# FFN up projections of a two-layer trunk: norm and block sums per tile on VectorE, weights by 128 columns two pairs ahead

## The chip, the cores and the metric

One NeuronCore of a Trainium2 chip runs the whole program. The metric is the device time of one execution in microseconds; the kernel before has a median of 2,806.35 us over three runs (2,805.0 to 2,806.55).

## The reference

The input is a residual stream of 1,024 tokens with 1,024 features, all float32. Layer 0 mixes tokens with multi-head latent attention (MLA), layer 1 with a gated MLP over chunks of 128 tokens (gMLP). Each is followed by a squared-ReLU feed-forward network (FFN) and a gated embedding (PLE):

```python
for i in range(DEPTH):                       # DEPTH = 2
    hn = rms_norm(h, norm_mix[i])
    mix = mla_mixer(hn, ...) if i == 0 else gmlp_mixer(hn, ...)
    h = h + mix                              # both end in a product with w_out
    hn = rms_norm(h, norm_ffn[i])
    h = h + jnp.square(jax.nn.relu(hn @ ffn_w_up[i])) @ ffn_w_down[i]
    hn = rms_norm(h, norm_ple[i])
    h = h + jax.nn.sigmoid(hn @ ple_w_gate[i]) * (p[i] @ ple_w_proj[i])
```

`ffn_w_up[i]` is 1,024 x 4,096, `mla_w_out` 1,024 x 1,024, `gmlp_w_out` 2,048 x 1,024. `rms_norm` divides by the root of the mean square over the features and multiplies by a gain.

## The kernel before

The residual stream stands feature-major: `h[k]`, k = 0 to 7, holds features 128k to 128k+127 of all 1,024 tokens (128 x 1024). Every product is made of three: both factors are split into a rounded part (`hi`, a cast on ScalarE, called ACT below) and the rest (`lo`, a subtraction on VectorE, DVE), and TensorE (PE) adds hi x hi, hi x lo and lo x hi. `split` does both halves; its cast is L111, its subtraction L112. The names of an operand end in h and l, those of weights are `wh` and `wl`.

**Output projections.** `down_slice` (L537) goes over four groups q of 256 output columns. `load_block` fetches the weights of a group (512 KB) and splits them, then two tiles f = 0, 1 of 128 columns are computed and added to `h[j]` in PSUM eviction on DVE (L545). Two of these calls feed an FFN: the second half of the MLA projection, `wo1` (results `wo10` to `wo17`), and the last slice of the gMLP projection, `go3` (results `go30` to `go37`). After each second tile `NormX.add_pair` (L275) makes what the up projection needs of it.

**Up projections.** They use a scheme of seven products for a 2 x 2 block product. The blocks of the right side are made from `h[2q]` and `h[2q+1]` times the gain, each cut into two halves of 512 tokens: `B11`, `B21`, `B22` and the combinations `T1` to `T4`, all split into hi and lo. GpSimd (POOL) makes one difference and adds the squares for the norm (L304) into `n_acc`. `rest` splits what of T3 and T4 isn't made early. The weights come as 16 pairs of 128 columns: `wino_weights` (L340) loads a pair as two blocks of 4 k tiles x 256 columns (`wx_r`, 512 KB each, pieces of 1,024 bytes), makes eight sums on POOL of 128x256 (L356, L359, L362, L365), and splits seven operands `wx_A..` and `wx_S..`. `wino_up` runs `pair(n)` for n = 0 to 15, with `run(i)` for product i of seven, each 12 matmuls; the results are called `f0u3g` and `f0u3y` for the first layer's pair 3. The banks are x and z (`g`) and y; a result is copied out of a bank on ACT (`u`, L443) before the next product is added to it. In pair 0 the sums of squares become the norm's factor: `nrm.sums` splits `n_acc` (`n_shl`, L209 and L210), PE adds it up over partitions (`f0u0st`), `nrm.roots` makes `n_rb`. Each finished row of 128 is stored to `apark` in DRAM and read back for the down projection.

**What sets the order.** Each engine has one queue which runs in order. A scheduler writes the queues out ahead of time, by the code's order, dependences, free slots in the pools (`pr` for raw weights, `pw` and `ph` for splits, `pt` for temporaries) and a lead `LEAD`. `up_first` draws the first operands of pair 0's weights while the projection ahead of it still runs (`after(j)`).

Of the kernel before, what the change touches and what calls it, by code (L numbers as in the profile page):

```python
# [40 lines left out]
def trunk(ctx: ExitStack, tc: tile.TileContext, I, out):  # L41
# [218 lines left out]
    class NormX(Norm):  # L260


        def __init__(self, name, gains, place, early):
# [6 lines left out]
        def put(self, c, q, src):  # L270
            hi, lo = self.place(self.name, c, q)
            split(hi, lo, src)
            self.x[c][q] = (hi, lo)

        def add_pair(self, q, h):  # L275
            n = f"{self.name}_{q}"
            u = [tmp(f"{n}u{e}", [P, 2, 512]) for e in range(2)]
            for e in range(2):
                S.activation(u[e].rearrange("p c t -> p (c t)"), h[2 * q + e], AF.Copy, scale=self.g[2 * q + e])
            a = tmp(f"{n}a", [P, 2, 512])  # L280
            b = pw.tile([P, 2, 512], F32, tag="w", name=f"{n}b")
            G.tensor_tensor(a[:, 0], u[0][:, 1], u[0][:, 0], op=ALU.subtract)
            V.tensor_tensor(b[:, 0], u[1][:, 1], u[0][:, 1], op=ALU.subtract)
            self.put("B21", q, u[1][:, 0])
            self.put("B11", q, u[0][:, 0])
            V.tensor_tensor(a[:, 1], u[1][:, 1], a[:, 0], op=ALU.subtract)
            self.put("T1", q, a[:, 0])
            V.tensor_tensor(b[:, 1], u[1][:, 0], a[:, 1], op=ALU.subtract)
            self.put("T2", q, a[:, 1])
            self.put("B22", q, u[1][:, 1])  # L290
            for c, src in (("T3", b[:, 0]), ("T4", b[:, 1])):
                if c in self.early:
                    self.put(c, q, src)
                else:
                    self.kept[c, q] = src
            for e in range(2):
                k = 2 * q + e
                if self.acc is None:
                    self.acc = pb.tile([P, T], F32, tag="acc", name=f"{self.name}_acc")
                    S.activation(self.acc, h[k], AF.Square)  # L300
                else:
                    sq = tmp(f"{n}sq{e}")
                    S.activation(sq, h[k], AF.Square)
                    G.tensor_tensor(self.acc, sq, self.acc, op=ALU.add)  # L304
                nc.sync.dma_start(self.hpark[k], h[k])

        def rest(self):
            for c in ("T3", "T4"):
                for q in range(4):
                    if (c, q) in self.kept:  # L310
                        self.put(c, q, self.kept.pop((c, q)))
# [26 lines left out]
    wslot = [0]  # L338

    def wino_weights(w, f0):  # L340
# [4 lines left out]
        for j in range(2):  # L345
            r = pr.tile([P, 4, 256], F32, tag="raw", name=f"{name}r{j}")
            nc.sync.dma_start(r, w[j * 512:(j + 1) * 512, f0:f0 + 256].rearrange("(k p) f -> p k f", p=P))
            raw.append(r.rearrange("p (q e) (g f) -> p q e g f", e=2, g=2))

        def quad(j, e, g):  # L350
            return raw[j][:, :, e, g, :]

        sa, sb = (ph.tile([P, 2, 4, 128], F32, tag="h", name=f"{name}s{x}") for x in "ab")
        for j in range(2):
            js = slice(2 * j, 2 * j + 2)
            G.tensor_tensor(sa[:, 0, js], quad(j, 0, 1), quad(j, 1, 1), op=ALU.add)  # L356
        for j in range(2):
            js = slice(2 * j, 2 * j + 2)
            G.tensor_tensor(sa[:, 1, js], sa[:, 0, js], quad(j, 0, 0), op=ALU.subtract)  # L359
        for j in range(2):  # L360
            js = slice(2 * j, 2 * j + 2)
            G.tensor_tensor(sb[:, 0, js], quad(j, 1, 0), sa[:, 1, js], op=ALU.subtract)  # L362
        for j in range(2):
            js = slice(2 * j, 2 * j + 2)
            G.tensor_tensor(sb[:, 1, js], quad(j, 0, 0), quad(j, 0, 1), op=ALU.subtract)  # L365
        for what in ("A12", "A11", "S1", "S2", "S4", "S3", "A22"):
            wslot[0] = (wslot[0] + 1) % 12
            pool, tag = (ph, "h") if wslot[0] % 12 < 4 else (pw, "w")
            t = pool.tile([P, 2, 4, 128], F32R, tag=tag, name=f"{name}{what}")
            if what[0] == "A":  # L370
                e, g = int(what[2]) - 1, int(what[1]) - 1
                for j in range(2):
                    js = slice(2 * j, 2 * j + 2)
                    split(t[:, 0, js], t[:, 1, js], quad(j, e, g))
            else:
# [1066 lines left out]
```

## Time and profile before

| | before |
|---|---|
| median of three runs | 2,806.35 us |
| profiled execution: time, span | 2,807.97 us, 2,806.2 us |
| TensorE (PE) matmul, busy | 2,654.2 us, 95% |
| VectorE (DVE) busy | 1,461.8 us, 52% |
| ScalarE (ACT) busy | 1,050.4 us, 37% |
| GpSimd (POOL) busy | 598.4 us, 21%, 738 instructions |
| mean granted TensorE clock | 0.975 |

The profiled execution is one run with the hardware profiler on; its time lies 1.8 us above its span, and it lies 1.6 us above the median of the others. Busy shares are means over the whole span. The strips of the page show each engine in 40 slices of the span, a digit being the busy share in tenths; PEclk is the clock that TensorE was granted, in tenths of full speed.

### The profile page before, as it was taken

What the parts mean: (1) busy time and instruction counts of PE and PEld (TensorE: products, weight loads), DVE (VectorE), ACT (ScalarE), POOL (GpSimd) and SP (SyncE); (2) the same over time, 40 slices, a digit from 0 to 9 for tenths busy, and PEclk for the clock granted to TensorE, in tenths of its full rate; (3) what the DMA queues carried; (4) which work ended last, traced back from release to release, by engine and by line L of the source; (5) the groups of instructions that cost most, each with busy time, mean ns of one, the idle gap of its engine ahead of it and who ended that gap; (6) DMA issues with size and microseconds to landing.
All of it is one profiled execution on the core that took longest, in us unless ns stands there. A gap on an engine that the chain in (4) does not pass through costs nothing. (4 is left out here: it accounts for less than half of the span.)

```text
span 2806.2 us, 34481 instructions
## 1 busy us (share of the span) xinstructions
PE 2654.2 (95%) x13216; PEld 2224.5 (79%) x13216; DVE 1461.8 (52%) x2336; ACT 1050.4 (37%) x2191; POOL 598.4 (21%) x738
## 2 busy tenths in 40 slices
PE   8999998689999999999999999995799999999999
PEld 7898986467777888888888787884577778888899
DVE  6777774565545444375523534435745555444652
ACT  4677762344434122154522221213543443211341
POOL 4544331342330000001211422213433310000000
PEclk9999999789999999999999999997899999999999
DMA  4100011123326333232233311311223254322221
GB/s 161 55 17 31 2 53 60 60 90 105 113 91 230 101 105 113 64 96 74 95 110 104 90 50 58 93 34 68 83 91 119 91 177 168 113 91 69 85 83 35
DMA packets 174262, 247.51 MB, mean 88 GB/s; under 512 B 9057, under 2 KB 135585, under 8 KB 174097
## 3 DMA queue, kind: packets, MB, share of 16 engines
q1 hardware_dynamic: 169280, 230.21, 25.2%
q0 software_dynamic: 4816, 15.10, 1.7%
q8 instruction: 104, 1.70, 0.3%
q14 instruction: 62, 0.50, 0.1%
HBM read 186.55 MB, written 58.72 MB: 87 GB/s over the span
## 5 line engine op out<-in xcount | busy, mean ns | idle before, releaser
L111 ACT CAST wh<-raw 128x1024 fp32r<-128x1024 f32 x96 | 101.0, 1052 | 321.7 <-PE f0d L65 115.9
L112 DVE TENSOR_TENSOR wx_A<-wx_r,wx_A 128x256 fp32r<-128x256 f32 x192 | 99.2, 552 | 116.9 <-ACT wx_A L111 116.2
L356 POOL TENSOR_TENSOR wx_sa<-wx_r 128x256 f32<-128x256 f32 x64 | 53.4, 835 | 454.7 <-DMA wx_r<-in_ffn_w_up_dram 301.0
L112 DVE TENSOR_TENSOR wl<-raw,wh 128x1024 fp32r<-128x1024 f32 x96 | 122.9, 1280 | 48.8 <-ACT wh L111 42.4
L545 DVE TENSOR_TENSOR f0h<-f0d,f0h 128x512 f32<-128x512 f32 (+1 forms) x84 | 70.3, 865 | 145.8 <-PE f0d L65 145.7
L545 DVE TENSOR_TENSOR f1h<-f1d,f1h 128x512 f32<-128x512 f32 (+1 forms) x84 | 70.3, 865 | 139.4 <-PE f1d L65 139.4
L614 POOL TENSOR_TENSOR f0h<-sig,f0h 128x512 f32<-128x512 f32 x16 | 21.9, 1387 | 487.4 <-DVE sig L613 470.2
L65 PE MATMUL go<-yh,wh 128*128 128x512 f32 x256 | 89.6, 418 | 22.6 <-ACT wh L111 22.6
L65 PE MATMUL go<-yh,wl 128*128 128x512 f32 x256 | 87.6, 409 | 9.3 <-DVE wl L112 9.3
L545 DVE TENSOR_TENSOR f0h<-go,f0h 128x512 f32<-128x512 f32 (+1 forms) x52 | 40.6, 810 | 103.4 <-PE go L65 103.4
L111 ACT CAST wx_A<-wx_r 128x256 fp32r<-128x256 f32 x192 | 70.9, 404 | 58.5 <-DMA wx_r<-in_ffn_w_up_dram 37.7
L764 ACT ACTIVATE u<-up,n_r 128x512 f32<-128x512 f32 x32 | 22.0, 688 | 189.1 <-PE up L65 189.1
L65 PE MATMUL go<-yl,wh 128*128 128x512 f32 x256 | 88.5, 413 | 0.0
L755 POOL TENSOR_TENSOR vr<-vr,gb 128x512 f32<-128x512 f32 x32 | 44.0, 1392 | 188.5 <-DVE vr L754 188.5
L694 DVE BATCH_NORM_STATS2 vst<-vg 128x6 f32<-128x512 f32 (+1 forms) x40 | 23.2, 586 | 110.5 <-ACT vg L693 110.5
L65 PEld LDWEIGHTS go<-yh,wh 128*128 128x128 f32 x256 | 51.3, 202 | 34.7 <-ACT wh L111 23.9
L65 PE MATMUL s<-kT,q 128*128 128x512 f32 (+5 forms) x288 | 73.1, 357 | 2.3 <-DVE q L112 1.8
L112 DVE TENSOR_TENSOR wx_S<-wx_sa,wx_S 128x512 fp32r<-128x512 f32 x64 | 56.1, 880 | 35.0 <-ACT wx_S L111 34.0
L693 ACT ACTIVATE vg<-vp,n_r 128x512 f32<-128x512 f32 (+1 forms) x40 | 23.8, 603 | 120.3 <-PE vp L65 118.9
L65 PE MATMUL av<-pt,v 128*128 128x256 f32 (+1 forms) x480 | 64.0, 283 | 5.0 <-DVE sm L1238 2.4
L1239 POOL TENSOR_SCALAR p<-p,sm 128x128 f32<-128x128 f32 (+3 forms) x64 | 49.2, 769 | 88.3 <-DVE sm L1238 58.1
L65 PEld LDWEIGHTS go<-yh,wl 128*128 128x128 f32 x256 | 50.5, 199 | 21.8 <-DVE wl L112 11.5
(5241 smaller groups left out, 8431.1 us busy)
## 6 DMA issues: line engine op xcount, KB each, us to landing
wx_r<-in_ffn_w_up_dram SPq DMA_DIRECT2D x64, 512.0 KB, 4.8
raw<-in_ffn_w_down_dram SPq DMA_DIRECT2D x56, 512.0 KB, 3.5
f0ar<-f_apark SPq DMA_DIRECT2D x32, 512.0 KB, 4.0
f1ar<-f_apark SPq DMA_DIRECT2D x32, 512.0 KB, 4.2
raw<-in_ffn_w_down_dram SPq DMA_DIRECT2D x32, 256.0 KB, 2.9
raw<-in_ple_w_gate_dram SPq DMA_DIRECT2D x16, 512.0 KB, 3.9
vr<-vpark SPq DMA_DIRECT2D x16, 512.0 KB, 4.0
raw<-in_gmlp_w_out_dram SPq DMA_DIRECT2D x16, 512.0 KB, 3.5
```

The source lines that it names most:

```text
L65: PE.matmul(o, l, r, start=start, stop=stop)
L111: S.copy(hi, src)
L112: V.tensor_tensor(lo, src, f32(hi), op=ALU.subtract)
L356: G.tensor_tensor(sa[:, 0, js], quad(j, 0, 1), quad(j, 1, 1), op=ALU.add)
L545: V.tensor_tensor(h[j][:, c], u, h[j][:, c], op=ALU.add)
L614: G.tensor_tensor(h[j][:, cs], sg, h[j][:, cs], op=ALU.add)
L693: last = S.activation(t, o, AF.Gelu_apprx_tanh, scale=nrm.r[:, b:b + 1])
L694: V.bn_stats(vst[:, b, cc], t)
L755: G.tensor_tensor(v, v, gb[:, 0], op=ALU.mult)
L764: S.activation(us[b][:, b % 2], o, AF.Gelu_apprx_tanh, scale=r[:, b:b + 1])
L1239: G.tensor_scalar(pr_[:, :n], pr_[:, :n], sm[:, 2:3], 1.0, op0=ALU.mult, op1=ALU.mult)
```

## The change

The squares, T3 and T4 leave the projection ahead of the FFN and go into pair 0. What stays is made after each tile, not after each two, and without POOL. The weights come as two loads of 8 k tiles x 128 columns (pieces of 512 bytes), their sums are four operations of 128x512 on DVE, and the load of pair n+2 is issued in pair n. `down_slice` loads the next 256 columns' weights after the first tile of the group ahead, if it feeds a norm. `pr` gets a fourth slot and `LEAD` goes from 304 to 16.

```diff
-LEAD = 304
+LEAD = 16
-    pr = ctx.enter_context(tc.tile_pool(name="pr", bufs=3))
+    pr = ctx.enter_context(tc.tile_pool(name="pr", bufs=4))
-        def add_pair(self, q, h):
...
+        def single(self, c, q, k, hk):
+            hi, lo = self.slot(c, q)
+            S.activation(hi, hk, AF.Copy, scale=self.g[k])
+            V.scalar_tensor_tensor(lo, hk, self.g[k], f32(hi), op0=ALU.mult, op1=ALU.subtract)
+        def add_tile(self, k, h):
+            q, g = k // 2, self.g[k]
+            nc.sync.dma_start(self.hpark[k], h[k])
+            h0, h1 = h[k][:, CS[0]], h[k][:, CS[1]]
+            if k % 2 == 0:
+                self.t = tmp(f"{self.name}_{q}t", [P, 2, 512])
+                t1 = self.t[:, 0]
+                S.activation(t1, h0, AF.Copy, scale=g)
+                V.scalar_tensor_tensor(t1, h1, g, t1, op0=ALU.mult, op1=ALU.subtract)
+                self.single("B11", q, k, h0)
+                split(*self.slot("T1", q), t1)
+            else:
+                t1, t2 = self.t[:, 0], self.t[:, 1]
+                self.single("B21", q, k, h0)
+                V.scalar_tensor_tensor(t2, h1, g, t1, op0=ALU.mult, op1=ALU.subtract)
+                split(*self.slot("T2", q), t2)
+                self.single("B22", q, k, h1)
+        def late_t3(self, q, h):
+            t = tmp(f"{self.name}_{q}t3")[:, :512]
+            S.activation(t, h[2 * q][:, CS[1]], AF.Copy, scale=self.g[2 * q])
+            V.scalar_tensor_tensor(t, h[2 * q + 1][:, CS[1]], self.g[2 * q + 1], t, op0=ALU.mult, op1=ALU.subtract)
+            split(*self.slot("T3", q), t)
+        def late_t4(self, q, h):
+            t = tmp(f"{self.name}_{q}t4")[:, :512]
+            th, tl = self.x["T2"][q]
+            V.scalar_tensor_tensor(t, h[2 * q + 1][:, CS[0]], self.g[2 * q + 1], f32(th), op0=ALU.mult, op1=ALU.subtract)
+            V.tensor_tensor(t, t, f32(tl), op=ALU.subtract)
+            split(*self.slot("T4", q), t)
+        def square(self, k, h):
+            if self.acc is None:
+                self.acc = pb.tile([P, T], F32, tag="acc", name=f"{self.name}_acc")
+                S.activation(self.acc, h[k], AF.Square)
+            else:
+                sq = tmp(f"{self.name}sq{k}")
+                S.activation(sq, h[k], AF.Square)
+                V.tensor_tensor(self.acc, sq, self.acc, op=ALU.add)
...
+        for g in range(2):
+            r = pr.tile([P, KT, P], F32, tag="raw", name=f"{name}r{g}")
+            nc.sync.dma_start(r, w[:, (2 * n + g) * P:(2 * n + g + 1) * P].rearrange("(k p) f -> p k f", p=P))
+            raw.append(r.rearrange("p (q e) f -> p q e f", e=2))
...
+            s1, s2 = sums("a")
+            V.tensor_tensor(s1, quad["A21"], quad["A22"], op=ALU.add)
+            yield put("S1", s1)
+            V.tensor_tensor(s2, s1, quad["A11"], op=ALU.subtract)
+            yield put("S2", s2)
+            s4, s3 = sums("b")
+            V.tensor_tensor(s4, quad["A12"], s2, op=ALU.subtract)
+            yield put("S4", s4)
+            V.tensor_tensor(s3, quad["A11"], quad["A21"], op=ALU.subtract)
+            yield put("S3", s3)
...
+            if n + 2 < nfp:
+                gens[n + 2] = wino_weights(w, n + 2)
...
             if n == 0:
                 for qs in (range(3), range(3, 4)):
                     for i in range(3):
                         run(i, qs)
-                scale(u)
+                while len(wt) < 5:
+                    prepare(0)
+                for q in range(2):
+                    nrm.late_t3(q, h)
...
+            if n == 0:
+                run(5)
+                for k in range(KT):
+                    nrm.square(k, h)
+                scale(u)
...
+            if n == 0:
+                while len(wt) < 7:
+                    prepare(0)
+                for q in range(4):
+                    nrm.late_t4(q, h)
...
     def down_slice(w, k0, rhs, h, name, nxt, seq=False, before=None, after=None):
+        bl = None
         for q in range(4):
-            bl = [load_block(w, k0, q * 256)]
+            bl, ahead = bl or [load_block(w, k0, q * 256)], None
...
-                if nxt is not None and j % 2:
-                    nxt.add_pair(j // 2, h)
+                if nxt is not None and f == 0 and q < 3:
+                    ahead = [load_block(w, k0, (q + 1) * 256)]
+                if nxt is not None:
+                    nxt.add_tile(j, h)
...
+            bl = ahead
```

In `up_first` the weights of pair 0 are created at j = 3 and three of their operands are made at j = 4, 5 and 6.

The queue of ACT during `wo1`, before: tiles 4 and 5 are done, `n1_2u..` are their products with the gain, `n1_2sq..` their squares, `wx6_..` the weights of pair 0, and `wh9` the weights of the last 256 columns.

```order
L279 ACTIVATE n1_2u0_6061<-h4_5426,gT_94 128x1024
L279 ACTIVATE n1_2u1_6062<-h5_5428,gT_94 128x1024
L111 CAST n1T1_1_6078<-n1_2a_6065 128x512
L111 CAST n1B212h_6069<-n1_2u1_6062 128x512
L111 CAST n1B22_5875<-n1_2u1_6062 128x512
L111 CAST n1B112h_6073<-n1_2u0_6061 128x512
L111 CAST n1T2_5872<-n1_2a_6065 128x512
L303 ACTIVATE n1_2sq0_6086<-h4_5426 128x1024
L303 ACTIVATE n1_2sq1_6090<-h5_5428 128x1024
L111 CAST wx6_S1_6094<-wx6_sa_5981 128x512
L111 CAST wh9_6099<-raw9_6097 128x1024
```

The same queue in the change, from the last cast of the attention's result (`oh71`) on; `n1_0t` is the first row of the norm's work on tile 0, and `wx7_..` are the weights of pair 0.

```order
L111 CAST oh71_5784<-O7_5269 128x512
L111 CAST wh6_5822<-raw6_5820 128x1024
L111 CAST wh7_5905<-raw7_5903 128x1024
L111 CAST wh9_5989<-raw9_5987 128x1024
L285 ACTIVATE n1_0t_5827<-h0_5418,gT_94 128x512
L275 ACTIVATE n1B110h_5830<-h0_5418,gT_94 128x512
L111 CAST n1T1_0_5834<-n1_0t_5827 128x512
L111 CAST wx7_A12_6004<-wx7_r0_5957 128x512
```

All three casts of the later column groups now stand ahead of the norm's first row, where `wh9` stood behind the work on tiles 4 and 5.

The queue of DVE in pair 0 of the first layer, before: `n10_shl` and `n11_shl` are the low parts of the two halves of `n_acc`, `n1T40l` to `n1T43l` the low parts of the last operand, and L237 and L238 belong to the root.

```order
L112 TENSOR_TENSOR wx6_A22_6230<-wx6_r1_5979,wx6_A22_6230 128x256
L210 TENSOR_TENSOR n10_shl_6279<-n1_acc_5878,n10_shl_6279 128x512
L112 TENSOR_TENSOR n1T33l_6208<-n1_3b_6165,n1T33h_6207 128x512
L210 TENSOR_TENSOR n11_shl_6285<-n1_acc_5878,n11_shl_6285 128x512
L112 TENSOR_TENSOR n1T40l_6212<-n1_0b_5856,n1T40h_6211 128x512
L112 TENSOR_TENSOR n1T41l_6216<-n1_1b_5950,n1T41h_6215 128x512
L112 TENSOR_TENSOR n1T42l_6220<-n1_2b_6066,n1T42h_6219 128x512
L112 TENSOR_TENSOR n1T43l_6224<-n1_3b_6165,n1T43h_6223 128x512
L237 SCALAR_TENSOR_TENSOR n10_vr_6293<-n10_vr_6293 128x512
```

The queue of DVE in pair 0 of the change, from the last T3 operand to the root; L316 adds a square into `n1_acc`, `wx10_..` are the weights of pair 2 and `n1_0t4` is the first half of T4.

```order
L112 TENSOR_TENSOR n1T33l_6217<-n1_3t3_6213,n1T33h_6216 128x512
L316 TENSOR_TENSOR n1_acc_6265<-n1sq1_6267,n1_acc_6265 128x1024
...
L112 TENSOR_TENSOR wx10_S1_6433<-wx10_sa_6431,wx10_S1_6433 128x512
L377 TENSOR_TENSOR wx10_sa_6431<-wx10_sa_6431,wx10_r0_6132 128x512
L210 TENSOR_TENSOR n10_shl_6289<-n1_acc_6265,n10_shl_6289 128x512
L210 TENSOR_TENSOR n11_shl_6295<-n1_acc_6265,n11_shl_6295 128x512
L112 TENSOR_TENSOR wx10_S2_6450<-wx10_sa_6431,wx10_S2_6450 128x512
L237 SCALAR_TENSOR_TENSOR n10_vr_6303<-n10_vr_6303 128x512
L238 SCALAR_TENSOR_TENSOR n1_rb_6300<-n10_vr_6303,n1_rb_6300 128x512
L477 TENSOR_TENSOR f0u0a1_6140<-f0u0g_6136,f0u0e_6138 128x512
L237 SCALAR_TENSOR_TENSOR n11_vr_6310<-n11_vr_6310 128x512
L305 SCALAR_TENSOR_TENSOR n1_0t4_6325<-h1_5420,gT_94,n1T2_5871 128x512
```

The seven additions of squares, which were POOL's, now stand on DVE ahead of the sums' low parts, and the T4 work, which stood ahead of the root, stands behind it.

## Rows read from the trace of the kernel before

**Rows 1.** The page: PE's line of the busy times, and PE's busy strip and granted clock in 40 slices.

```profile
PE 2654.2 (95%) x13216; PEld 2224.5 (79%) x13216; DVE 1461.8 (52%) x2336; ACT 1050.4 (37%) x2191; POOL 598.4 (21%) x738
...
PE   8999998689999999999999999995799999999999
...
PEclk9999999789999999999999999997899999999999
```

**Rows 2.** Busy time of each engine (with its instructions) in six stretches: length, PE, PE's weight load, DVE, ACT, POOL, granted clock, DMA share, GB/s. The first three stretches are `wo1`, pair 0 and pairs 1 to 15 of the first layer, the last three `go3` without its first column group, pair 0 and pairs 1 to 15 of the second.

```profile
461.00:549.00 88.00, 54.35 (x195) 41.72 (x195) 44.11 (x46) 26.72 (x37) 29.81 (x21) 0.75 0.16 60
549.00:594.00 45.00, 29.84 (x108) 21.41 (x107) 37.62 (x51) 29.82 (x55) 23.51 (x18) 0.81 0.21 71
594.00:903.00 309.00, 300.52 (x1269) 233.27 (x1268) 159.64 (x238) 125.82 (x237) 85.62 (x100) 0.99 0.37 125
1905.00:1982.00 77.00, 45.07 (x149) 33.97 (x148) 44.00 (x44) 25.81 (x39) 30.43 (x21) 0.71 0.17 63
1982.00:2028.00 46.00, 30.63 (x115) 22.35 (x114) 39.49 (x53) 29.52 (x56) 21.97 (x18) 0.89 0.24 81
2028.00:2331.00 303.00, 296.12 (x1257) 229.87 (x1256) 153.73 (x232) 125.15 (x233) 84.61 (x100) 1.00 0.36 125
```

**Rows 3.** Waits of PE from 455 to 620 us, by what was waited for: us in total, times, longest.

```profile
PE wo L65 <- ACT wh L111: 24.1, 3, 8.4
PE wo L65 <- DVE wl L112: 9.5, 3, 3.6
PE f0u1y L389 <- ACT wx_A L111: 5.7, 1, 5.7
PE f0u0st L65 <- ACT n_shl L209: 5.0, 2, 4.8
```

**Rows 4.** The same from 1,900 to 2,030 us.

```profile
PE go L65 <- ACT wh L111: 22.6, 3, 9.7
PE go L65 <- DVE wl L112: 9.3, 3, 3.9
PE f1u1y L389 <- ACT wx_A L111: 4.8, 1, 4.8
```

**Rows 5.** The same from 600 to 910 us, the first and the last of five rows.

```profile
PE f0u11g L389 <- ACT f0u11u L443: 2.2, 1, 2.2
...
PE f0u4g L389 <- ACT f0u4u L443: 1.0, 1, 1.0
```

**Rows 6.** PE in order of time: start, duration, instruction, and in brackets the idle time ahead of it with what ended it. Stretches of `wo1`, of the borders of pair 0 and of the loop, then of `go3` and the second layer's borders.

```profile
461.04 0.62 PE L65 MATMUL wo<-oh,wh 128*128 128x512 f32 x2
...
479.43 1.22 PE L65 MATMUL wo<-oh,wh 128*128 128x512 f32 x2 [7.34 <-ACT wh L111]
...
548.75 0.39 PE L389 MATMUL f0u0y<-n1B210h,wx_A 128*128 128x512 f32 x1
...
593.25 0.39 PE L389 MATMUL f0u1g<-n1B111l,wx_A 128*128 128x512 f32 x1
593.48 0.39 PE L389 MATMUL f0u1g<-n1B111h,wx_A 128*128 128x512 f32 x1
593.71 0.39 PE L389 MATMUL f0u1g<-n1B112h,wx_A 128*128 128x512 f32 x1
...
902.89 0.39 PE L65 MATMUL f0d<-f0a000l,wh 128*128 128x512 f32 x1
...
1904.96 0.61 PE L65 MATMUL go<-yh,wl 128*128 128x512 f32 x2
...
1981.64 0.39 PE L389 MATMUL f1u0y<-n4B210h,wx_A 128*128 128x512 f32 x1
...
2027.90 2.88 PE L389 MATMUL f1u1g<-n4T,wx_S 128*128 128x512 f32 x12
...
2330.64 0.39 PE L65 MATMUL f1d<-f1a031h,wh 128*128 128x512 f32 x1
```

**Rows 7.** ACT in order of time in `wo1`, from the first row of the norm's work on tiles 0 and 1 to the cast of the next weights.

```profile
473.22 1.15 ACT L279 ACTIVATE n_0u<-h,gT 128x1024 f32<-128x1024 f32 x1 [3.18 <-DVE h L545]
...
478.33 1.04 ACT L111 CAST wh<-raw 128x1024 fp32r<-128x1024 f32 x1
```

**Rows 8.** DVE in order of time: two operations of 128x512 in a row with POOL idle, and two of 128x256 beside POOL; and POOL's row of that time.

```profile
526.72 0.68 DVE L286 TENSOR_TENSOR n_2a<-n_2u,n_2a 128x512 f32<-128x512 f32 x1
527.32 0.68 DVE L112 TENSOR_TENSOR n1B212l<-n_2u,n1B212h 128x512 fp32r<-128x512 f32 x1
...
504.49 5.08 DVE L112 TENSOR_TENSOR wx_A<-wx_r,wx_A 128x256 fp32r<-128x256 f32 x2
...
503.32 5.96 POOL L304 TENSOR_TENSOR n_acc<-n_1sq,n_acc 128x1024 f32<-128x1024 f32 x2 [7.59 <-ACT n_1sq L303]
```

**Rows 9.** The page's DMA issues: queue, count, size of one, median us from issue to landing.

```profile
wx_r<-in_ffn_w_up_dram SPq DMA_DIRECT2D x64, 512.0 KB, 4.8
...
raw<-in_ple_w_gate_dram SPq DMA_DIRECT2D x16, 512.0 KB, 3.9
```

**Rows 10.** Groups of instructions from 600 to 905 us, pairs 1 to 15 of the first layer: busy us and mean ns of one, then idle time ahead and its releaser.

```profile
L112 DVE TENSOR_TENSOR wx_A<-wx_r,wx_A 128x256 fp32r<-128x256 f32 x78 | 38.0, 521 | 54.5 <-ACT wx_A L111 54.1
L112 DVE TENSOR_TENSOR wx_S<-wx_sa,wx_S 128x512 fp32r<-128x512 f32 x26 | 22.1, 849 | 18.7 <-ACT wx_S L111 18.3
...
L359 POOL TENSOR_TENSOR wx_sa<-wx_sa,wx_r 128x256 f32<-128x256 f32 x25 | 23.0, 921 | 1.1
```

More of the change, by code (lines that the diff above doesn't have):

```diff
@@ L260, in trunk, with __init__ @@
     class NormX(Norm):
-        def __init__(self, name, gains, place, early):
+        def __init__(self, name, gains, place):
             super().__init__(name, gains)
-            self.place, self.early = place, early
-            self.x = {c: [None] * 4 for c in ("B11", "B12", "B21", "B22", "T1", "T2", "T3", "T4")}
-            self.kept = {}
+            self.place = place
+            self.x = {c: [None] * 4 for c in ("B11", "B21", "B22", "T1", "T2", "T3", "T4")}
             self.hpark = pd.tile([KT, P, T], F32, name=f"{name}_hpark")
[L270 to L273, printed above, removed]
@@ L275, in add_pair @@
-        def add_pair(self, q, h):
[L276 to L311, printed above, removed]
+        def slot(self, c, q):
+            self.x[c][q] = self.place(self.name, c, q)
+            return self.x[c][q]
+        def single(self, c, q, k, hk):
+            hi, lo = self.slot(c, q)
+            S.activation(hi, hk, AF.Copy, scale=self.g[k])
+            V.scalar_tensor_tensor(lo, hk, self.g[k], f32(hi), op0=ALU.mult, op1=ALU.subtract)
@@ L344, in wino_weights @@
         raw = []
[L345 to L375, printed above, removed]
-                src = {"S1": sa[:, 0], "S2": sa[:, 1], "S4": sb[:, 0], "S3": sb[:, 1]}[what]
-                split(t[:, 0], t[:, 1], src)
-            yield t
+        for g in range(2):
+            r = pr.tile([P, KT, P], F32, tag="raw", name=f"{name}r{g}")
+            nc.sync.dma_start(r, w[:, (2 * n + g) * P:(2 * n + g + 1) * P].rearrange("(k p) f -> p k f", p=P))
+            raw.append(r.rearrange("p (q e) f -> p q e f", e=2))
@@ new lines, in wino_weights, with new, put, sums @@
+        quad = {f"A{g + 1}{e + 1}": raw[g][:, :, e, :] for g in range(2) for e in range(2)}
+        count = [0]
+        def new(what):
+            m = 7 * n + count[0]
+            count[0] += 1
+            pool, tag = (ph, "h") if m >= 14 and m % 12 < 4 else (pw, "w")
+            return pool.tile([P, 2, 4, P], F32R, tag=tag, name=f"{name}{what}")
+        def put(what, src):
+            t = new(what)
+            split(t[:, 0], t[:, 1], src)
+            return t
+        def sums(x):
+            pool, tag = (pb, {"a": "acc", "b": "rb"}[x]) if n == 0 else (ph, "h")
+            s = pool.tile([P, 2, 4, P], F32, tag=tag, name=f"{name}s{x}")
+            return s[:, 0], s[:, 1]
@@ L465, in last @@
                 out(2 * n + 1, row[1].rearrange("p c t -> p (c t)"))
-            return nxt, ready, last
-        gen, ready = first
+            return last
         late = None
         for n in range(nfp):
-            gen, ready, late = pair(n, gen, ready, late)
+            late = pair(n, late)
         late()
@@ L1157, in mla @@
             block_x(1)
-            pf = pm.tile([NB, P], F32, name="posf")
+            pf = tmp("posf")[:NB, :P]
             V.tensor_copy(pf, pi)
@@ L1409, in trunk @@
     last = ple_out(1, hf, n5)
-    ffn(1, n4, n5, lambda: next(last), (gen, ready), hf)
+    ffn(1, n4, h, n5, lambda: next(last), (gen[0], ready), hf)
     next(last, None)
```

87 lines of the change are left out of this document (46 added, 41 removed).

## The prediction

> **What bounds the kernel now.** I read the strips of the page first [rows 1]: TensorE (PE) is busy 95% of the span, and its busy strip has two dents, slices 7 to 9 and 28 to 29, where the granted clock falls too. A slice is a fortieth of 2,806.2 us, 70 us, so the dents lie within 420 to 630 and 1,890 to 2,040 us. Cutting those stretches at the borders of the code [rows 2] shows the second half of the MLA output projection (461 to 549: PE busy 54.35 of 88 us, clock 0.75), the first pair of the first up projection (549 to 594: 29.84 of 45, clock 0.81), its other fifteen pairs (300.52 of 309, clock 0.99), and the same three places of the second layer. Work that PE must do is there in all six; only in two of them is PE really full.
>
> The waits name the causes. Around the first dent PE waits 24.1 us for `wh` casts on ScalarE (ACT) and 9.5 us for `wl` on VectorE (DVE), three each; then 5.7 us for a weight split of the second pair and 5.0 us for the sums of squares [rows 3]. Around the second it waits 22.6 and 9.3 us for `wh` and `wl`, and 4.8 us for the split [rows 4]. From pair 1 on only small waits for an eviction on ACT are left, five rows from 2.2 to 1.0 us, 8.2 in all for the first layer [rows 5].
>
> To price a dent I compare its length with its matmuls at full speed, 0.2267 us apart (593.25, 593.48, 593.71 [rows 6]). From 461.04 to 548.75 are 87.7 us for 192 matmuls (43.5 at full speed): 44.2 lost, of which 33.6 are waits and 10.6 matmuls at the lower clock behind each wait (1.22 us for two against 0.62 [rows 6]). In go3 the three later column groups take 1905.4 to 1981.64, 76.2 us for 144 matmuls (32.6): 43.6 lost, 31.9 of them waits. Pair 0 takes 44.5 us for 104 matmuls in the first layer (23.6): 20.9 lost; in the second 46.26 for 114 (25.8): 20.4 lost. Pairs 1 to 15 take 309.64 us for some 1,270 matmuls (287.9): 21.7 lost; in the second 302.74 for some 1,254 (284.3): 18.5 lost. Together 169 us lie open here. What the change can move lies in these places.
>
> Why `wh` is late is seen on ACT [rows 7]: the cast at 478.33 stands behind the gain, the casts and a square of the finished pair of tiles, which began at 473.22 only when PE's last result had been evicted. The cast's own row has no idle time ahead of it, so it did not wait for its raw block: it is place in the queue, not the transfer.
>
> **The change, part by part.**
>
> *Next weights ahead of the norm's work.* In the order, `wh7` and `wh9` move ahead of all of the norm's rows on ACT, and `wl` likewise on DVE. So the waits of 33.6 and 31.9 us go, and with them the slow clock behind each. Is there cover? The new work per 256 columns on DVE is two tiles' evictions (2.4 us, four halves of 0.60), seven 128x512 operations of the splits, one `wl` (twice 0.60) and one or two weight splits or sums. At 0.60 apart (526.72 to 527.32 [rows 8]) that is 9 to 10 us, against 48 matmuls x 0.2267 = 10.9 us on PE. It fits narrowly; with the cover gone PE would wait for what is over, 1 or 2 us a group. I take 1 us left in each projection: -43 and -42.6. In go3 the casts move ahead of the last activations of the gMLP (u37, yh37), where PE ends the gating products; two 1.04 us casts ahead of them delay the last `yl` by some 2 us (bounds 0 and 4), so -42.6 + 2.1 = -40.5.
>
> *Norm per tile and no POOL.* The subtractions become two-input operations with the gain inside, still one DVE operation of 0.60 each; the removed POOL operations were beside the path, apart from what they took from DVE. A DVE operation beside POOL's takes longer: two of 128x256 took 5.08 us beside the 5.96 us of POOL's sum of squares, 0.68 alone for one of 128x512 [rows 8].
>
> *Sums, squares and T4 within pair 0.* DVE's rows from the eviction of the last tile to the last T4 split are 58: 50 of 128x512 x 0.60 = 30, 8 of 128x1024 at 1.14 (about twice 0.60) = 9.1, together 39.2; the root chain through ACT leaves about 4.6 us open, a little under the 5.0 that PE waits for it now. So the last T4 operand is ready 43.8 us after the projection ends. PE has 129 matmuls to that point (29.2 us), for it now takes pair 1's y and x products ahead of T4. Its loss is 14.6, some 1.5 behind it and 3 at the lower clock: 19 against 20.9. I take -2 in each layer. Bounds: +8, if the chain through the squares (ACT square, DVE add, seven times in turn) is not closed up, and -7, if weight work slips behind it.
>
> *Weights by 128 columns, sums on DVE.* Eight POOL sums of 128x256 become four on DVE, and the 128x256 splits become single 128x512 ones. DVE per pair: 7 splits + 4 sums = 11 x 0.60 = 6.6, evictions, relu and squares some 4: 10.7 of the 20.6 us that a pair takes now (309.64/15). That stays hidden under PE. With two pairs' lead the casts no longer stand in ACT's queue for a POOL sum, so half of the 8.2 us of eviction waits [rows 5] should go: -4 and -3.5; bounds 0 and all of the 21.7 and 18.5.
>
> *Loads.* The number of bytes is the same, the piece is 512 bytes instead of 1,024. The up weights land in 4.8 us, the gate weights, 512 KB in pieces of 512 bytes, in 3.9 [rows 9]. Both lie far under a pair's 20.6 us: nothing.
>
> Sum: -43 - 40.5 - 2 - 2 - 4 - 3.5 = -95 from the profiled execution's 2,807.97 us: 2,713. The median lies 1.6 below the profiled execution, so 2,711.
>
> **The rivals.**
>
> A, the forecast: the two projections become full, pair 0 about as bad as now. 2,690 to 2,730.
>
> B, the stall moves from the projections into pair 0. DVE then has 39 us of work in a stretch in which PE has 29, and all queue for one engine. If the root chain comes late (each of the seven adds waits for its square, whose slot waits for the add two before) by 1.5 us each, pair 0 is 10 to 15 longer in each layer: 2,711 + 25 = 2,736. For it speaks that DVE is already the fuller one here (37.62 of 45 us [rows 2]), against it that POOL no longer slows it.
>
> C, the interference with POOL was worth more than its rows. In pairs 1 to 15 the splits' means are 521 ns for 128x256 and 849 for the S splits where 680 is the plain price, with POOL's 921 beside them [rows 10]. Over the first layer's loop that is some 12 (78 x 0.15) + 4 + 1 = 17 us of DVE time of 160 [rows 2], and DVE is not what PE waits for. If DVE's and ACT's queues run free of it nevertheless, all of the 40 us lost in the two loops goes instead of 7.5: 2,711 - 33 = 2,678.
>
> The Trainium skill, page "SBUF — State Buffer", section "Who interferes with whom", says that VectorE and GpSimd contend for one shared port pair as an exclusive lock, that the one which comes second blocks fully, and ("SBUF: two separate sides") that an operation of VectorE with two SBUF inputs is concerned when GpSimd reads SBUF. By that up to all of POOL's 85.6 us in the loop would be taken from DVE. The trace agrees with the blocking in the row of 5.08 us; the loop's rows give a fifth of it.
>
> D, the change doesn't do it: the casts stand early in the queue but their raw blocks land late, since a load must wait for a slot that the block before still holds. Then the 65.5 us of weight waits and their slow clock stay: 2,711 + 87 = 2,798. Four slots instead of three and landing times of 3.5 to 5 us against 10.9 us of matmuls speak against it.
>
> E, slower: the loads of half-sized pieces become the pace. Per pair two loads and two stores of 512 KB go through one queue. If pieces of half the size take twice the time, two loads are 2 x 9.6 and two stores 2 x 4.8, 28.8 us against 20.6, and 30 pairs add 246: 2,957. It turns the sign from loads of (20.6 + 95/30 - 9.6)/2 = 7.1 us on, were they one after the other. The gate's 3.9 us at 512 bytes, and a DMA share of 0.37 in the loop [rows 2], speak against it.
>
> The Trainium skill, page "DMA: Bandwidth & Descriptors", section "Specifications", gives 512 bytes as the smallest transfer for the full line rate, and the new piece stands right at that edge; by that the price is nothing, as taken.
>
> **How the numbers follow.** A 0.60, B 0.15, C 0.13, D 0.05, E 0.05, nothing at all 0.02. The range, 2,683 to 2,745, holds A and B with a pair 0 that is a few us worse, and reaches close to C; C's lower part, D and E are outside. Faster by over 0.2% (5.6 us, about what a measurement of this kernel can tell from no change) are A to D: 0.93; same 0.02; slower 0.05.
>
> **What the profile of the changed kernel would show.** The two dents of PE and its clock shrink to one slice each; no `wo` or `go` row waits for `wh` or `wl` over 1 us; the second half of the MLA projection takes 44 to 46 us. In pair 0 PE's longest wait is now for a T4 split or the root, 10 to 15 us in sum; pair 0 takes 40 to 50. The loop's eviction waits fall under 5 us. POOL loses its sums, DVE gains some 40 us in number but not in busy time. Wrong would be: waits for `wh` that stay (D), load rows over 7 us with PE waiting for A12 casts (E), or a pair 0 over 55 us (B).

## The result and the profile after

The change takes 2,694.23 us (median of four, 2,692.13 to 2,698.71) against 2,805.86 us of the kernel before on the same chip: a ratio of 0.9604 with an interval of 0.9588 to 0.9621, 111.6 us less. The forecast was 2,711, in a range of 2,683 to 2,745. The profiled execution of the change is its fastest (2,692.13 us) and lies 115.8 us under that of before; the sums below are made against it.

The page of the change, PE's line and strips:

```profile
PE 2622.8 (97%) x13216; PEld 2208.6 (82%) x13216; DVE 1481.4 (55%) x2398; ACT 1040.0 (39%) x2095; POOL 322.8 (12%) x460
...
PE   7999999999999999999999999999899999999999
...
PEclk9999999999999999999999999999899999999999
```

Of the two dents of [rows 1] one slice is left, with an 8 in both strips. (The 7 at the very start is the kernel's first slice, an 8 before.) The same six stretches as in [rows 2], at the borders they now have (the last products of pair 0 end at 552.3 and 1,925.3 us):

```profile
462.00:506.00 44.00, 44.00 (x195) 36.43 (x195) 32.42 (x46) 20.56 (x32) 0.00 (x0) 1.00 0.29 108
506.00:552.30 46.30, 35.55 (x128) 25.57 (x127) 41.73 (x60) 31.49 (x49) 0.00 (x0) 0.89 0.10 35
552.30:842.60 290.30, 290.30 (x1244) 228.18 (x1243) 173.97 (x254) 125.12 (x200) 0.00 (x0) 1.00 0.42 135
1845.00:1878.00 33.00, 33.00 (x148) 27.31 (x147) 27.22 (x40) 17.63 (x28) 0.00 (x0) 1.00 0.30 113
1878.00:1925.00 47.00, 37.12 (x132) 27.07 (x131) 42.26 (x61) 31.74 (x49) 0.00 (x0) 0.85 0.10 34
1925.00:2215.00 290.00, 289.08 (x1237) 226.39 (x1236) 170.15 (x249) 123.25 (x198) 0.00 (x0) 1.00 0.42 136
```

Both projections are full, 44.00 of 44 and 33.00 of 33 us at full clock, and PE has next to no idle time in the loops either. Only the two pairs 0 are not full. What PE waits for in the first of them (455 to 600 us, the four longest of seven waits, 10.9 us in all; [rows 3] before):

```profile
PE f0u0st L65 <- ACT n_shl L209: 4.0, 1, 4.0
PE f0u0g L397 <- ACT n1T40h L111: 2.1, 1, 2.1
PE f0u0g L397 <- ACT n1T41h L111: 1.9, 1, 1.9
PE f0u0g L397 <- DVE n1T40l L112: 1.2, 1, 1.2
```

No `wo` row and no `go` row waits for a weight; from 552 to 842 us the list of PE's waits is empty. The borders, which answer to [rows 6]:

```profile
462.28 0.61 PE L65 MATMUL wo<-oh,wh 128*128 128x512 f32 x2
...
505.80 0.39 PE L397 MATMUL f0u0y<-n1B210h,wx_A 128*128 128x512 f32 x1
...
552.33 0.39 PE L397 MATMUL f0u0g<-n1T43h,wx_A 128*128 128x512 f32 x1
...
842.64 0.39 PE L65 MATMUL f0d<-f0a031l,wh 128*128 128x512 f32 x1
...
1877.73 0.39 PE L397 MATMUL f1u0y<-n4B210h,wx_A 128*128 128x512 f32 x1
```

From such borders, with the matmuls between them counted in the order of the program and 0.2267 us each, one gets the time lost in each place (the loops here end at the start of their last matmul, and `go3` begins among the last of the gMLP's own matmuls, at 1,895.0 and 1,835.0):

| us | before | forecast of the difference | after | difference |
|---|---|---|---|---|
| start to `wo1` | 461.0 | 0 | 462.3 | +1.2 |
| `wo1`, lost | 44.2 | -43 | 0 | -44.2 |
| pair 0 of layer 0, lost | 20.9 | -2 | 17.5 | -3.4 |
| pairs 1 to 15, lost | 21.7 | -4 | 8.5 | -13.2 |
| from there to `go3`, time | 992.4 | +2.1 | 992.5 | +0.2 |
| `go3`, time | 86.6 | -42.6 | 42.8 | -43.8 |
| pair 0 of layer 1, lost | 20.4 | -2 | 17.4 | -3.0 |
| pairs 1 to 15, lost | 18.5 | -3.5 | 10.1 | -8.4 |
| the rest | 475.8 | 0 | 475.1 | -0.7 |

The 8.5 and 10.1 us that stay in the loops are hardly waits (0 and 0.9 us). Where a product is added to a bank that holds another, its first two matmuls take longer, as at 643.26:

```profile
643.00 0.39 PE L397 MATMUL f0u6g<-n1B113l,wx_A 128*128 128x512 f32 x1
643.26 0.50 PE L397 MATMUL f0u5g<-n1T40h,wx_A 128*128 128x512 f32 x1
643.60 0.39 PE L397 MATMUL f0u5g<-n1T40l,wx_A 128*128 128x512 f32 x1
```

From 643.00 to 643.60 are 0.60 us for two matmuls in place of 0.45. Four of a pair's seven products begin so, 60 in a loop: by these rows an estimate of 9 us. So of the 169 us that the prediction held to be open, some 18 never were.

### The profile page after: what moved, and what is told of

It is laid out like the page before. It is cut to its first block, busy times and chain, and to the rows that moved or that the text cites. A ratio compares the mean times of both kernels' runs of the same rounds, so it can differ in the third digit from the quotient of the medians.

```text
span 2690.3 us, 34099 instructions
## 1 busy us (share of the span) xinstructions
PE 2622.8 (97%) x13216; PEld 2208.6 (82%) x13216; DVE 1481.4 (55%) x2398; ACT 1040.0 (39%) x2095; POOL 322.8 (12%) x460
## 3 DMA queue, kind: packets, MB, share of 16 engines
q1 hardware_dynamic: 202048, 230.21, 26.6%
## 4 chain that ended last, share of the span: by engine, by line
PE 84%; DVE 6%; ACT 4%; DMA 1%; issue 1%; POOL 0%; DVEq 0%; ACTq 0%; SPq 0%; POOLq 0%
PE f0d L65 13%; PE f1d L65 13%; PE vp L65 7%; PE up L65 6%; PE go L65 6%; PE e L65 4%; PE wo L65 3%; PE pg L65 3%; PE s L65 2%; PE pq L65 1%; PE av L65 1%; PE pj L65 1%; PE sv L65 1%; PE pk L65 1%; PE f0u10g L397 1%
## 5 line engine op out<-in xcount | busy, mean ns | idle before, releaser
L112 DVE TENSOR_TENSOR wx_A<-wx_r,wx_A 128x512 fp32r<-128x512 f32 x96 | 65.3, 688 | 82.3 <-ACT wx_A L111 82.1
L65 PE MATMUL go<-yh,wh 128*128 128x512 f32 x256 | 83.8, 391 | 0.0
L65 PEld LDWEIGHTS av<-pt,v 128*128 128x128 f32 x480 | 59.9, 191 | 8.2 <-issue 3.8
L111 ACT CAST wx_A<-wx_r 128x512 fp32r<-128x512 f32 x96 | 58.4, 620 | 16.6 <-DVE wx_S L112 4.8
L1271 POOL TENSOR_SCALAR p<-p,sm 128x128 f32<-128x128 f32 (+3 forms) x64 | 49.5, 773 | 86.6 <-DVE sm L1270 54.3
L65 PE MATMUL f0d<-f_ah,wh 128*128 128x512 f32 x192 | 59.2, 389 | 0.0
L65 PE MATMUL f1d<-f_ah,wh 128*128 128x512 f32 x192 | 59.2, 389 | 0.0
L65 PE MATMUL f1d<-f_ah,wl 128*128 128x512 f32 x192 | 59.1, 389 | 0.0
L65 PE MATMUL f0d<-f_ah,wl 128*128 128x512 f32 x192 | 59.1, 389 | 0.0
```

What stands on the lines that cost most here:

```text
L65: PE.matmul(o, l, r, start=start, stop=stop)
L111: S.copy(hi, src)
L112: V.tensor_tensor(lo, src, f32(hi), op=ALU.subtract)
L1271: G.tensor_scalar(pr_[:, :n], pr_[:, :n], sm[:, 2:3], 1.0, op0=ALU.mult, op1=ALU.mult)
```

## The experiments

Theory 1 was that the projections gain because the weights are fetched ahead of the norm's work, and the loops because POOL's sums are gone. The rivals: the lighter work of the norm is enough by itself; and the loops gain by when their weights come.

Lost time in each run, worked out as above (`go3`: time over 42.8). Each median stands beside the ratio to the kernel before on the same chip:

| run | median, ratio [interval] | wo1 | pair 0 | loop | go3 | pair 0 | loop |
|---|---|---|---|---|---|---|---|
| before | | 44.2 | 20.9 | 21.7 | 43.8 | 20.4 | 18.5 |
| e2 before, early fetch | 2747.84, 0.9805 [0.979, 0.9819] | 8.7 | 24.2 | 23.0 | 10.8 | 26.1 | 19.9 |
| e5 before, 4 raw slots | 2782.44, 0.9936 [0.9921, 0.995] | 42.9 | 18.7 | 12.2 | 42.5 | 14.6 | 10.3 |
| the change (e9) | 2694.41, 0.9615 [0.9602, 0.9628] | 0 | 17.4 | 8.6 | 0 | 16.8 | 10.1 |
| e1 no early fetch | 2694.2, 0.9612 [0.9598, 0.9627] | 0 | 17.5 | 8.7 | 0 | 17.3 | 10.8 |
| e12 two tiles together | 2691.84, 0.9601 [0.9582, 0.9621] | 0 | 17.4 | 8.9 | 0 | 16.9 | 9.9 |
| e3 sums on POOL | 2729.61, 0.9743 [0.9727, 0.9759] | 0 | 31.3 | 13.9 | 0 | 30.2 | 11.9 |
| e4 one pair ahead | 2693.05, 0.9611 [0.9597, 0.9626] | 0 | 17.1 | 9.2 | 0 | 17.8 | 9.6 |
| e6 T4, then squares | 2715.73, 0.9705 [0.9689, 0.9721] | 0 | 9.4 | 30.0 | 0 | 8.5 | 29.3 |
| e7 squares early | 2690.98, 0.9606 [0.9592, 0.962] | 0 | 13.6 | 10.4 | 0 | 14.1 | 10.1 |
| e8 the same on POOL | 2706.94, 0.9665 [0.9651, 0.968] | 0 | 20.2 | 11.1 | 0 | 24.9 | 9.2 |
| e10 root, then T4 | 2683.56, 0.9578 [0.9565, 0.9591] | 0 | 10.5 | 10.0 | 0 | 10.0 | 10.5 |
| e11 T3, root, T4 | 2678.65, 0.9557 [0.9544, 0.9571] | 0 | 8.0 | 9.5 | 0 | 7.7 | 9.6 |

### e1: the change without the early fetch

```diff
-                if nxt is not None and f == 0 and q < 3:
-                    ahead = [load_block(w, k0, (q + 1) * 256)]
```

> The changed kernel, but down_slice fetches each 256 columns' weights at the start of their own group. Theory 1 (the projections gain because the fetch is written ahead of the norm's work): wh and wl waits come back in part, 40 to 85 us more than the change, 2,735 to 2,780. Theory 2 (they gain because the norm's work per tile is lighter, needs no POOL and frees the queues and slots): within 10 us of the change, 2,690 to 2,705, with at most one wh wait per projection.

The change stays as it is, 0.9612 against 0.9615. Theory 1 falls as it stood. In the change itself ACT casts the weights of the three later groups before `wo1` begins at 462.28, each when PE has left a block of the first half of the projection:

```profile
440.26 1.05 ACT L111 CAST wh<-raw 128x1024 fp32r<-128x1024 f32 x1 [5.92 <-PE wo L65]
451.14 1.06 ACT L111 CAST wh<-raw 128x1024 fp32r<-128x1024 f32 x1 [9.82 <-PE wo L65]
462.02 1.05 ACT L111 CAST wh<-raw 128x1024 fp32r<-128x1024 f32 x1 [9.82 <-PE wo L65]
```

Without the early fetch only the last of the three moves, to 471.67, which is early enough too.

### e2: the kernel before with the early fetch alone

The lines of `down_slice` as in the change, with `add_pair` kept.

> The kernel before, with down_slice's early fetch alone. Theory 1: the six wh waits go and with them the slow clock behind them, 2,806 - 70 to 88, that is 2,718 to 2,736. Theory 2: the norm's work for two tiles at once still fills ACT and DVE, so at least half of the waits stay: 2,765 or more.

53.4 us less than before (2,801.28 on that chip). The `wh` waits go, but for one of 1.2 us in `go3`. Of `wo1`'s 44.2 us lost 8.7 stay, as waits for `wl` and the slow clock behind them. `wl` stands in DVE's queue behind the norm's work and the weights of pair 0, and DVE is slow there beside POOL's squares (6.04 us from 488.91 on):

```profile
482.83 0.73 PE L65 MATMUL wo<-oh,wl 128*128 128x512 f32 x2 [2.00 <-DVE wl L112]
497.49 1.22 PE L65 MATMUL wo<-oh,wl 128*128 128x512 f32 x2 [3.48 <-DVE wl L112]
...
491.20 4.03 DVE L112 TENSOR_TENSOR wx_A<-wx_r,wx_A 128x256 fp32r<-128x256 f32 x2
495.15 2.28 DVE L112 TENSOR_TENSOR wl<-raw,wh 128x1024 fp32r<-128x1024 f32 x1
```

68 us come out of the two projections, and some 9 go back into the pairs 0, where the norm's work then piles up. So the fetch alone does about three quarters of it where the norm's work is heavy, and does nothing where that is light. Neither number that the two theories gave was met.

### e12: two tiles at once

```diff
-                if nxt is not None:
-                    nxt.add_tile(j, h)
+                if nxt is not None and j % 2:
+                    nxt.add_tile(j - 1, h)
+                    nxt.add_tile(j, h)
```

The early fetch is left out here too.

> The changed kernel without the early fetch, and with the work of two tiles done together after the second, as before; what is done per tile, and on which engine, stays the change's. If making the norm's operands tile by tile is what fills the projections: waits for wh or wl come back, 10 us or more per projection, 2,715 or more. If it is that this work no longer goes through POOL, holds no weight slots (the kernel before keeps four tiles of T3 and T4 in the pool pw) and has no squares in it, so that the casts stand ahead of it in ACT's queue in either case: within 5 us of the change, pair 0 some 2 us longer because the last two tiles are done late.

No different from the change (0.9601 against 0.9615, the intervals overlap), and pair 0 isn't longer, as was expected. Neither the early fetch nor the step from pairs to tiles is needed: what is left of the change in the projections is that the norm's work has no POOL step, no squares, and no tiles that stay in `pw`, and that three of pair 0's weight operands are made there and not five. The squares are not it by themselves: in e7 and e8, which keep the early fetch, they are back in the projection, added on DVE and on POOL, and nothing is lost there. Which of the others puts the casts ahead in ACT's queue was not separated.

### e3: the block sums back on POOL

```diff
-            V.tensor_tensor(s1, quad["A21"], quad["A22"], op=ALU.add)
+            G.tensor_tensor(s1, quad["A21"], quad["A22"], op=ALU.add)
```

and so the other three sums.

> The changed kernel with its four block sums per pair on POOL in place of DVE. If the loops' gain of 20 us over my sum for them and before came from taking POOL's work away (it slows DVE and makes ACT's casts wait): waits for evictions on ACT come back in pairs 1 to 15, 12 to 20 us more than the change, 2,706 to 2,715, and DVE's splits of 128x512 take longer than 690 ns. If it came from the loads two pairs ahead or from the larger splits: within 4 us of the change.

35 us slower than the change, more than expected, but elsewhere: the pairs 0 lose 13.8 and 12.8 us more, the loops 5.4 and 1.8. Two things are seen there. First DVE and POOL at 542 us, both at operations that read two tiles in SBUF:

```profile
542.00 1.75 DVE L306 TENSOR_TENSOR n_0t<-n_0t,n1T 128x512 f32<-128x512 f32 x1
543.68 2.28 DVE L471 SCALAR_TENSOR_TENSOR f0u0a<-f0u0a,n_rb 128x1024 f32<-128x1024 f32 x1
545.88 1.75 DVE L478 SCALAR_TENSOR_TENSOR f0u0a<-f0u0a,n_rb 128x512 f32<-128x512 f32 x1
547.56 1.75 DVE L112 TENSOR_TENSOR n1T40l<-n_0t,n1T40h 128x512 fp32r<-128x512 f32 x1
...
541.56 3.31 POOL L380 TENSOR_TENSOR wx_sb<-wx_r,wx_sa 128x512 f32<-128x512 f32 x2 [11.70 <-DVE n_0t L305]
544.84 3.92 POOL L382 TENSOR_TENSOR wx_sb<-wx_r,wx_r 128x512 f32<-128x512 f32 x2
```

Four operations that take 0.69, 1.22, 0.69 and 0.69 in the change take 1.75, 2.28, 1.75 and 1.75, each 1.06 longer: they alternate with POOL's four. That agrees with what the Trainium skill says (page "SBUF — State Buffer", "SBUF: two separate sides"): the second one blocks until the first is through. Six of DVE's operations in pair 0 are held up like this, 6.4 us in all, beside 18.2 us of POOL: a good third of POOL's time comes out of DVE's. Second, a queue behind POOL:

```profile
558.61 0.62 ACT L111 CAST wx_S<-wx_sa 128x512 fp32r<-128x512 f32 x1 [6.12 <-POOL wx_sa L377]
...
562.22 0.61 ACT L111 CAST n1T43h<-n_3t 128x512 fp32r<-128x512 f32 x1
...
562.88 0.80 PE L397 MATMUL f0u0g<-n1T43h,wx_A 128*128 128x512 f32 x1 [7.29 <-ACT n1T43h L111]
```

The last T4 operand was made on DVE at 555.43 to 556.1; its cast stands in ACT's queue behind the cast of a weight sum that waits for POOL, and PE waits 7.29 us.

### e4: one pair ahead

```diff
-            if n + 2 < nfp:
-                gens[n + 2] = wino_weights(w, n + 2)
+            if n + 1 < nfp:
+                gens[n + 1] = wino_weights(w, n + 1)
```

> The changed kernel with each pair's weights loaded one pair ahead, not two. If the lead of two pairs is what freed ACT's queue in the loops: 10 to 20 us more than the change, 2,704 to 2,714, with ACT's casts waiting for a load. If it was POOL's absence: within 4 us of the change.

No difference (0.9611 against 0.9615). The second pair of lead is worth nothing here.

### e5: the kernel before with a fourth raw slot

```diff
-    pr = ctx.enter_context(tc.tile_pool(name="pr", bufs=3))
+    pr = ctx.enter_context(tc.tile_pool(name="pr", bufs=4))
```

Three more edits make room, all of them in the change too: `LEAD` is 16, the copy of a bank goes to `e0` in place of a tile of its own, and a small tile moves to the temporaries. (`LEAD` is the width of a tile that POOL zeroes at the start of the program, L81; 288 columns less are 1,152 bytes of each partition.) They were not run without the slot.

The idea came from the kernel before in pair 11, where PE waited longest in the loop [rows 5]. POOL, ACT and PE in order of time there:

```profile
804.98 0.74 POOL L356 TENSOR_TENSOR wx_sa<-wx_r 128x256 f32<-128x256 f32 x1 [14.42 <-DMA wx_r<-in_ffn_w_up_dram]
...
808.12 0.62 ACT L111 CAST wx_S<-wx_sb 128x512 fp32r<-128x512 f32 x1 [2.78 <-POOL wx_sb L362]
808.64 0.58 ACT L443 COPY f0u11u<-f0u11g 128x512 f32<-128x512 f32 x1
...
809.27 4.60 PE L389 MATMUL f0u11g<-n1B,wx_S 128*128 128x512 f32 x12 [2.17 <-ACT f0u11u L443]
```

A block of weights lands late, POOL makes four sums from it, ACT's cast waits for them, and the copy of a bank behind the cast comes when PE has waited 2.17 us; behind the wait the twelve matmuls take 4.60 us, at the lower clock, where 2.72 is full speed. The load, the second of pair 13's two, was issued at 800.41, behind the store of a finished row in the DMA queue:

```profile
793.59 6.39 SPq L484 DMA_DIRECT2D f_apark<-f0u10a  x2
800.41 12.29 SPq L347 DMA_DIRECT2D wx_r<-in_ffn_w_up_dram  x4
```

With three slots and two loads for a pair there is never room for two whole pairs, and the order puts the second load of a pair that much later. Some loads also wait in the queue itself; from 594 to 905 us it has

```profile
SPq L347 <- DVE wx_A L112: 40.7, 14, 10.1
```

fourteen loads that waited for a split to leave a slot.

> The kernel before with a fourth slot for raw weights, room for it made by the lead of 16, by the copy of a bank in e0 in place of its own tile, and by one small tile placed among the temporaries. If the loops' eviction waits of the kernel before came from loads that wait for a slot (ACT's casts and POOL's sums stood behind a late load in pairs 1, 6 and 11): the loops lose 8 to 13 us less in each layer, 2,801 - 16 to 26, 2,775 to 2,785. If they came from POOL's eight sums or the half-width splits: within 5 us of the kernel before.

18.5 us less than before, and the loops lose 12.2 and 10.3 in place of 21.7 and 18.5, with POOL's eight sums and the half-width splits as they were. PE's waits from 590 to 905 us are down to

```profile
PE f0u1g L389 <- DVE f0u1a L435: 1.2, 1, 1.2
PE f0u14g L389 <- DVE f0u14a L445: 0.8, 1, 0.8
```

What went with them are POOL's waits for a load, from 594 to 890 us in the kernel before and in e5:

```profile
POOL wx_sa L356 <- DMA wx_r<-in_ffn_w_up_dram: 135.1, 12, 22.1
...
POOL wx_sa L356 <- DMA wx_r<-in_ffn_w_up_dram: 16.8, 2, 9.0
```

The loads still wait for slots, thirteen of them for 32.6 us in e5, but they come early enough: in pairs 3 to 15 the second load of a pair is issued 33 us or more ahead of the pair's first product, where it was 18 to 31.

### e6: T4 ahead of the squares

In pair 0 the eviction of T3's product and `late_t4` stand ahead of `square` and `scale`.

> The changed kernel, in pair 0 with the T4 operands made ahead of the squares and the root. If PE's wait for T4 is only its place in DVE's queue: T4's 12 matmuls follow T3's at once, the sums come 8 us later but PE has pairs 1 and 2 to do by then; 3 to 8 us less per layer, 2,678 to 2,688. If the root is what binds (the rows of pair 0 hold the temporaries until it is there): within 4 us of the change.

21 us slower. T4's product does come early (pair 0 loses 9.4), but the sums come too late, and PE waits for them with everything that the unscaled rows hold up behind it:

```profile
PE f0u0st L65 <- ACT n_shl L209: 10.5, 1, 10.5
```

The sums now stand behind the last product of pair 0, so the loop has that wait and loses 30.0. So the root binds as much as T4.

### e7 and e8: the squares in the projection

```diff
                 self.single("B22", q, k, h1)
+            self.square(k, h)
...
+                scale(u)
                 while len(wt) < 5:
...
-                for k in range(KT):
-                    nrm.square(k, h)
-                scale(u)
```

The sums of pair 0's blocks share one tile, so that `n_acc` has its own. e8 adds the squares on POOL.

> The changed kernel with the squares in add_tile of the projection, still added on DVE, and the root at the start of pair 0 (the block sums of pair 0 share one tile to make room). DVE's 39 us of pair 0 lose 8; in the projection they must fit beside its 32 of 43.5 us. If DVE's amount of work in pair 0 is what binds: 6 to 10 us less per layer, 2,674 to 2,682. If the squares push weight casts or evictions back in the projection: waits for wh or wl come back there, 2,694 or more.

> As the run with early squares on DVE, but POOL adds them. If an operation of POOL blocks DVE for only a part of its time: the same gain or 2 us more, 2,670 to 2,682. If POOL blocks DVE for most of its time (seven additions of 3 us each are 21 us of a 43.5 us stretch in which DVE is busy for 32): DVE falls behind in the projection and PE waits there or in pair 0, 2,690 to 2,710.

e7: the projection stays full with DVE 37.6 of 44 us busy, the pairs 0 lose 3 to 4 us less. Its interval holds the change's 0.9615, so by its time alone it is no faster. What PE waits for is now a copy behind the root's chain on ACT, and T4:

```profile
PE f0u0g L403 <- ACT f0u0e L460: 3.3, 1, 3.3
PE f0u0g L403 <- ACT n1T40h L111: 1.9, 1, 1.9
```

e8: no wait in the projection here either, but pair 0 loses 6.6 and 10.8 more than with DVE adding. POOL takes 2.4 to 4.8 us for an addition where DVE takes 1.22, and in the first layer the last one ends 12.5 us into pair 0, in e7 5.6.

### e9, e10 and e11: what pair 0 can still give

e9 is the change again. e10 and e11 are e7 with all T4 operands right behind T3's, ahead of the eviction of the first rows. e10 has the root after the first two copies, ahead of the second half of T3, e11 after all of T3, as here:

```diff
                 for q in range(2, 4):
                     nrm.late_t3(q, h)
+                scale(u)
+                for q in range(4):
+                    nrm.late_t4(q, h)
```

> The changed kernel itself, beside the two versions with the squares in the projection, so that a few us can be compared on one chip: a ratio to the kernel before of 0.959 to 0.962.

> The squares are added on DVE in the projection, the root stands behind the first copies of pair 0 and all T4 operands right behind T3's, ahead of the eviction of the first rows. If pair 0 is bound by what stands ahead of T4 in DVE's queue: T4's operands are there when T3's product ends, pair 0 loses 8 to 10 us in place of 17.5, 10 to 16 us less than the change on the same chip. If weight work of pairs 1 and 2, which stands between, binds as before: within 5 us.

> As the run with the root ahead of T4, but with the root behind all of T3. If ACT's root chain ahead of the copies costs the 3.3 us wait seen with early squares on DVE: 2 to 5 us less than the run with the root first; if the late root holds the rows back as it did with T4 ahead of the squares: equal or more.

e11 takes 2,678.65 us, 15.8 less than the change on the same chip, and its interval lies clear of the change's: it beats the kernel before and the change. The pairs 0 lose 8.0 and 7.7. e10 gains 10.9, and e11 some 5 more by the root's place, as expected; but e10 no longer has the wait of 3.3 us that this was expected of, its longest in pair 0 is 6.8 for the cast of the last T4 operand. In e11 one wait over 1 us is left in the first layer's pair 0:

```profile
PE f0u0g L403 <- DVE f0u0a L483: 5.4, 1, 5.4
```

## Why the prediction was right, point by point

**The bound and the two dents.** Right: PE's lost time in six places was the whole of it, and 116.0 us of the 169 came from there, against 115.8 for the whole kernel. What the 169 took for open and wasn't are the loops' 8.5 and 10.1 us, which stay in the change with hardly a wait.

**The next weights ahead of the norm's work.** The sizes were right: -43 forecast and -44.2 measured, -42.6 and -43.8; the cover held, and with more room than forecast (DVE busy 32.4 of 44 us). What the forecast took from the order was right too, the casts' place in ACT's queue. That the early fetch puts them there is wrong for the change (e1) and right for the kernel before (e2): the size came out although the part of the change that was named isn't the one that does it. Rival D is out.

**The gMLP's tail.** Forecast +2.1. PE does wait 1.8 us for a `yl`, as one row of the page shows, where it waited 0.0 before:

```profile
L65 PE MATMUL go<-yl,wh 128*128 128x512 f32 x256 | 83.8, 393 | 1.8 <-DVE yl L112 1.8
```

The stretch from the first layer's loop to `go3` is 0.2 longer. Between the profiled runs its length goes from 990.7 to 996.1 us though hardly anything differs in it, so that the 1.8 can't be told from it.

**Pair 0.** Forecast -2 each, measured -3.4 and -3.0. The step held: the last T4 operand was forecast 43.8 us after the projection; its split ends at 550.75, 44.95 after 505.80. The total came nearer than its parts: forecast were 14.6 us of waiting and 4.5 beside it, the rows have 10.9 of waiting and 6.6 beside it, for the most part matmuls at the lower clock (0.89 granted over the stretch). Rival B didn't come. e7 to e11 show its mechanism at work all the same: less ahead of T4 on DVE makes pair 0 shorter.

**Pairs 1 to 15: the step that was mis-sized.** "Half of the 8.2 us" gave -4 and -3.5; measured are -13.2 and -8.4. Two things failed. The waits went whole, 8.2 us to 0 and 6.9 to 0.9. In pair 11 the trace shows their chain: a load that comes late for want of a fourth raw slot, and with it POOL, ACT's cast and the copy behind it; the fourth slot, with the room made for it, takes the waits for an eviction on ACT away and gives -9.5 and -8.2 in the kernel before (e5). What gave the other 3.7 us in the first layer was not separated. I had named the copies' place behind POOL's sums, not the slot, and had put the loss to the two pairs' lead, which does nothing (e4). And with each wait goes the slow clock behind it, which I had counted in the projections and not in the loops: 5.0 and 2.4 us went there beside the waits.

**POOL, rival C.** It took the two loops at 33 us more, which would have needed the 18.6 us that stay in the change. The runs have 7.2 us in the loops and 26.6 in the pairs 0 for the sums on POOL (e3): the size was near, the place was not. e3 and e5 can't be added up, perhaps because a late POOL and a late load wait in the same queue; that was not tested. From rows of the loop alone I had 17 us of DVE time and no price where it counted: in pair 0, where DVE is the fuller engine, each blocked operation is on the path.

**Loads by 512 bytes, rival E.** They got no slower:

```profile
wx_r<-in_ffn_w_up_dram SPq DMA_DIRECT2D x64, 512.0 KB, 4.1
```

4.1 us against 4.8 [rows 9], though what made them shorter no run separates; that the smallest full-rate piece is 512 bytes, as the Trainium skill has it (page "DMA: Bandwidth & Descriptors", "Specifications"), agrees with this.

The sum missed 20.8 us against the profiled execution: 14.1 in the loops, 2.4 in the pairs 0, 2.4 in the projections, 1.9 in the tail.

## What to carry to other kernels

Where an engine's queue runs in order, look behind a small wait for the first thing that was late, not for the last: the copy that PE waited for stood behind a cast, that behind POOL's sums, those behind a load, and the load came late for want of a slot; one more slot, with the room made for it, was worth 18.5 us. A remedy must be tried alone and left out alone: the early fetch is worth 53 us in the kernel before and nothing in the change. When a stall is cleared, count the slow clock behind it as well: 13.2 us went from the first layer's loop, and 8.2 of them were waits.
